# Result buffers, the order of additions and two small tables in a mixture-of-experts kernel

## The chip, the cores and the metric

One core of a Trainium2 chip runs the kernel. Its engines work side by side, each through its own instructions in order: TensorE (PE; the weight loads of its array are listed apart as PEld), VectorE (DVE), ScalarE (ACT), GpSimd (POOL) and SyncE (SP, which issues transfers). Sixteen DMA engines move data between the device memory and the on-chip memory. The metric is device time in microseconds (us), the median of several runs; less is better.

## The reference

A decoder layer over 1024 tokens of 1024 channels: a mixer (gated linear attention and a state-space layer side by side), then a mixture of experts in which each token goes to 4 of 32 experts. What the change touches is the second part:

```python
def moe_ffn(h, router_w, router_b, w_gu, b_gu, w_down, b_down):
    logits = (xt @ router_w + router_b)
    top_val, top_idx = lax.top_k(logits, TOP_K)            # 4 of 32
    gate = jax.nn.softmax(top_val, axis=-1)
    ...                                                    # tokens sorted by expert
    def expert_block(args):
        xblk, e = args
        gu = xblk @ w_gu[e] + b_gu[e]
        g, up = gu[:, :D_FF], gu[:, D_FF:]
        g = jnp.minimum(g, SWIGLU_LIMIT)
        up = jnp.clip(up, -SWIGLU_LIMIT, SWIGLU_LIMIT)
        act = (up + 1.0) * (g * jax.nn.sigmoid(SWIGLU_ALPHA * g))
        return act @ w_down[e] + b_down[e]
    yb = lax.map(expert_block, (xb, block_e)).reshape(cap, D_)
    out = jnp.zeros((N + 1, D_), f32).at[tok_buf].add(yb * w_buf[:, None])[:N]
```

The last line is the one to keep in mind: a token's result is the sum of four experts' results, each times its gate.

## The kernel before, in words

**Stages.** Up to about 600 us: mixer, router, and a list of tokens and gates for each expert in device memory. From 613 to 1957 us: the experts. After that the sums are read back, normalised and added to the input.

**Experts.** Each expert has a capacity that is fixed when the program is built, by the rank of its load (`CAPS`); blocks are of up to 128 of its tokens. The 32 experts are taken in eight groups of four. Of each group first the gate and up products run, 32 chunks of weights of 1 MB each, then the down products, 16 chunks. SP loads a chunk into one of six staging buffers; ScalarE makes its high f16 half (`split_hi`, L1585), VectorE its low half (`split_lo`, L1588), into one of seven slots. TensorE multiplies the high half by the high and the low half of the tokens (L1791, L1792) and the low half by the high one (L1800). Every VectorE split also writes one column of check values, `gacc`, and so do the splits of tokens (L148); L1894 adds the columns up at the end.

**Tokens.** POOL gathers a block's rows through its list (L1726, an indirect transfer from `hn_d`); TensorE transposes them (L1736), VectorE and ScalarE evict them as f16 halves. A group's tokens are fetched during the down products of the group before.

**Results.** The down products give results with channels on the partitions. `out_jobs` treats one block and one half of the channels (c = 0 or 1): TensorE transposes four tiles into one of two PSUM banks (L1759); ScalarE (L1602) or VectorE (L143) evicts the bank, times the gate, into one of the buffers `yt_r` (tile A7, so A in the rows); POOL issues an indirect transfer that adds the buffer's rows to the sums `ff_d[c]` in device memory (L1765). There are 102 such additions. A buffer is free when its addition has landed; an addition is ordered behind all earlier ones to the same `ff_d[c]`.

**The general path.** An expert with more tokens than its capacity is finished by a loop after the experts, which is not entered with this input. Two tables that say what that loop would have to do (`overflow_table`, L1478 to L1507) are made by some 17 small VectorE operations and three small products each, ahead of the first expert. At the very end of the expert stage `gacc` is reduced, the table entries are read by the engines and the loop's branch is not taken. Then the sums are loaded (L1980).

**What sets the order.** All the work of the expert stage is written as jobs. A `Job` has the engines that can do it with a cost each, a due number, the jobs that it must follow, and a lag (time between the end of its cost and its result). `run_jobs` is a greedy planner that runs when the program is built: it repeatedly takes the job that can start first, and among equals the one with the earliest due number, gives it to the engine that suits, and writes its instructions. So a change of costs, lags or of what a job follows changes the order of the instructions on all engines.

Of the kernel before, what the change touches and what calls it, by code (L numbers as in the profile page):

```python
# [17 lines left out]
OP = mybir.AluOpType  # L18
AX = mybir.AxisListType
# [29 lines left out]
def hybrid_layer_kernel(ctx: ExitStack, tc: tile.TileContext, I, out):  # L49
# [73 lines left out]
    def trb(*dims):  # L123
        return bank("tr", 2, *dims)
# [525 lines left out]
    def take(gen, n=1):  # L650
        for _ in range(n):
            try:
                next(gen)
            except StopIteration:
                return
# [680 lines left out]
    spacer = small(1)  # L1336
# [139 lines left out]
    ov, nb, starts, jf_, om, ent = small(32), small(32), small(32), small(1), small(32), small(2)  # L1476

    def overflow_table(i, cap):  # L1478
        nbt = view(63, 32, 8)
        if cap is None:  # L1480
            V.tensor_copy(ov, cr[:, 0:32])
        else:
            sub(ov, cr[:, 0:32], cap)
        tt(V, nbt, bc(ov, 2, 8), bc(k128, 1, 32), OP.is_gt)
        V.tensor_reduce(nb, nbt, axis=AX.X, op=OP.add)
        V.tensor_tensor_scan(ov, ones[:, 0:32], nb, 0.0, OP.mult, OP.add)
        sub(starts, ov, nb)
        tt(V, om, starts, ecol.to_broadcast([128, 32]), OP.is_le)
        tt(V, nb, ov, ecol.to_broadcast([128, 32]), OP.is_gt)
        mul(om, om, nb)  # L1490
        if cap is None:
            ts(starts, starts, -128.0, OP.mult)
        else:
            stt(starts, starts, -128.0, cap, OP.mult, OP.add)
        mul(nb, om, cr[:, 32:64])
        V.tensor_reduce(ent[:, 0:1], nb, axis=AX.X, op=OP.add)
        mul(nb, om, starts)
        V.tensor_reduce(ent[:, 1:2], nb, axis=AX.X, op=OP.add)
        stt(ent[:, 1:2], ecol, 128.0, ent[:, 1:2], OP.mult, OP.add)
        V.tensor_reduce(jf_, om, axis=AX.X, op=OP.add)  # L1500
        mul(ent[:, 1:2], ent[:, 1:2], jf_)
        yield
        pe3 = trb(130)
        for q in range(2):
            PE.matmul(pe3[0:1, 64 * q:64 * q + 64], ent[0:64, q:q + 1], ident[0:64, 0:64], start=True, stop=True)
        PE.matmul(pe3[0:1, 128:129], jf_, ones[:, 0:1], start=True, stop=True)
        V.tensor_copy(otf[0:1, i, 0:129], pe3[0:1, 0:129])  # L1507

    e2, e3 = slot("E2"), slot("E3")
# [9 lines left out]
        WL.append(carve(t_, 4, 4, 256).bitcast(F16))  # L1519
    NST, NWS = len(ST), len(WH)  # L1520
    a7 = slot("A7")
    yt_r = [carve(a7, 2 * i, 512) for i in range(3)]
    gacc = carve(a7, 6, 500)
    V.memset(gacc, 0.0)
    gs_r, u_t = [carve(e2, 0, 1024), carve(e2, 4, 1024)], carve(e3, 0, 1024)
    CG = max(sum(CAPS[r] for r in g) for g in GROUPS)
    XKB = CG * 32 / 1024
    X0, A0, Y0, XG0 = 0, XKB, 2 * XKB, 2 * XKB + 2 * CAPS[0] / 64
    assert XG0 + 12 <= 64, XG0
    xg_r = Ring([XG0, XG0 + 4, XG0 + 8], 1024)  # L1530
    n_acc = [0]
    NBS = [(c_ + 127) // 128 for c_ in CAPS]
# [1 line left out]
    RS = 1.0 / (WS * XS)  # L1534

    def acc_col():
        n_acc[0] += 1
        return gacc[:, n_acc[0] - 1:n_acc[0]]

    class Expert:  # L1540
        pass
# [206 lines left out]

    ot_free, yt_free, added, n_ot = [None] * 2, [None] * len(yt_r), [None] * 2, [0]

    def out_jobs(x, c, b, yT, due, after):
        cb = min(128, x.C - 128 * b)
        q, y = n_ot[0] % 2, n_ot[0] % len(yt_r)
        n_ot[0] += 1
        pt, yt = ot_[q], yt_r[y]

        def transpose(e):
            for k in range(4):
                PE.transpose(pt[0:cb, k], yT[:, k, 128 * b:128 * b + cb], ident)  # L1759
        t_ = Job({"PE": 0.46}, due, after + [ot_free[q]], transpose)  # L1760
        ot_free[q] = Job({"ACT": act_us(512, True), "DVE": dve_us(512)}, due + 2, [t_, yt_free[y]],
                         lambda e: scaled(e, yt[0:cb], pt[0:cb].rearrange("p a b -> p (a b)"),
                                          x.lt[0:cb, b, 1:2].bitcast(F32)))
        yt_free[y] = added[c] = Job({"POOL": 1.7}, due, [ot_free[q], added[c]],
                                    lambda e: P.indirect_dma_start(  # L1765
                                        out=ff_d[c], out_offset=bass.IndirectOffsetOnAxis(ap=x.lt[0:cb, b, 0:1], axis=0),
                                        in_=yt[0:cb], in_offset=None, compute_op=OP.add), lag=7.0)
        return t_


# [4 lines left out]
    def sub_jobs(i, kind, x, c, js, n):  # L1775
# [62 lines left out]
        else:  # L1838
# [13 lines left out]
            ev = Job({"ACT": act_us(nj * C, True, nj), "DVE": dve_us(nj * C, nj)}, due, [end] + wait, results)  # L1852
            evs.append(ev)
            if js[-1] == 3:
                place[2].extend(out_jobs(x, c, b, yT, due + 2, list(evs)) for b in range(x.NB))
                y_used.append(place)
        for q in bi:
            bank_free[q] = ev
# [3 lines left out]
    load_list(ex[GROUPS[0][0]])  # L1862
    biases()
    tables = [overflow_table(0, capr), overflow_table(1, None)]
    for t_ in tables:
        take(t_, 2)
    tr_ += [trb(4, 128) for _ in range(2)]
    flat = [(ex[r], b) for r in GROUPS[0] for b in range(NBS[r])]
    for n in range(2):
# [6 lines left out]
    for i, u in enumerate(subs):  # L1876
        while made < min(len(chunks) + 5, u[4] + 2):
            chunk_jobs(made)
            made += 1
        if i_ph % 2 and i_ph < len(phase) - 1 and phase[i_ph][1] == i:  # L1880
            todo = [(ex[r], b) for r in GROUPS[i_ph // 2 + 1] for b in range(NBS[r])]
            span_ = 2 * (phase[i_ph + 1][1] - i)
            for k, (x, b) in enumerate(todo):
                token_jobs(x, b, 2 * i + (span_ - 4) * k / len(todo), [ld[phase[i_ph - 1][0]], step[0]])
        if i_ph < len(phase) and phase[i_ph][1] <= i:
            i_ph += 1
        sub_jobs(i, *u)
    while made < len(chunks) + 5:
        chunk_jobs(made)
# [129 lines left out]
```

## Time and profile before

| | us |
|---|---|
| median of 3 runs (2018.4 to 2021.25) | 2021.15 |
| profiled execution | 2024.69 |
| its span, first to last instruction | 2022.9 |
| busy: PE, DVE, ACT, POOL | 1806.0, 1544.2, 1199.1, 526.5 |
| mean granted clock of TensorE, share of full speed | 0.948 |
| 102 additions, POOL's issue of them, in all | 260.7 |
| VectorE's low split of a chunk | 2.29 |
| ScalarE's high split of a chunk | 1.92 |

The profiled execution is one run, 0.2% above the median; what is read from its rows is set against its own time. Busy times of engines overlap, so they can't be added. What tells where an edit is felt is the idle time of an engine and what ended it, stage by stage.

### The profile page before, as it was taken

What the parts mean: (1) busy time and instruction counts of PE and PEld (TensorE: products, weight loads), DVE (VectorE), ACT (ScalarE), POOL (GpSimd) and SP (SyncE); (2) the same over time, 40 slices, a digit from 0 to 9 for tenths busy, and PEclk for the clock granted to TensorE, in tenths of its full rate; (3) what the DMA queues carried; (4) which work ended last, traced back from release to release, by engine and by line L of the source; (5) the groups of instructions that cost most, each with busy time, mean ns of one, the idle gap of its engine ahead of it and who ended that gap; (6) DMA issues with size and microseconds to landing.
All of it is one profiled execution on the core that took longest, in us unless ns stands there. A gap on an engine that the chain in (4) does not pass through costs nothing. (4 is left out here: it accounts for less than half of the span.)

```text
span 2022.9 us, 53263 instructions
## 1 busy us (share of the span) xinstructions
PE 1806.0 (89%) x22354; PEld 1614.5 (80%) x22354; DVE 1544.2 (76%) x2396; ACT 1199.1 (59%) x1682; POOL 526.5 (26%) x495
## 2 busy tenths in 40 slices
PE   8678699998968999998998899999899889999970
PEld 3566588787858999998998899767799789999870
DVE  5766537568767997995997799689799868869835
ACT  3524133544226876875776677577688667768641
POOL 4720012203543025015104402400330330160043
PEclk8889899999978999999999899999999989999985
DMA  9176465323359999999999899888999999999874
GB/s 310 39 193 132 137 196 161 126 70 131 115 172 326 363 322 353 379 351 307 323 329 358 278 351 341 279 323 301 299 367 365 301 296 330 327 318 350 306 192 175
DMA packets 296804, 540.82 MB, mean 267 GB/s; under 512 B 41234, under 2 KB 66032, under 8 KB 296528
## 3 DMA queue, kind: packets, MB, share of 16 engines
q1 hardware_dynamic: 259504, 469.51, 67.5%
q0 software_dynamic: 30384, 60.49, 11.8%
q10 hardware_dynamic: 6672, 7.38, 1.1%
q8 instruction: 177, 2.90, 0.6%
q14 instruction: 67, 0.55, 0.1%
HBM read 489.57 MB, written 45.61 MB: 265 GB/s over the span
## 5 line engine op out<-in xcount | busy, mean ns | idle before, releaser
L1765 POOL DMA_INDIRECT ff_d<-A,S x102 | 260.7, 2555 | 353.8 <-DVE A L143 141.2
L1588 DVE SCALAR_TENSOR_TENSOR B<-A,B 128x2048 f16<-128x2048 f32 x110 | 249.5, 2285 | 33.1 <-ACT B L1585 21.0
L1588 DVE SCALAR_TENSOR_TENSOR E<-A,E 128x2048 f16<-128x2048 f32 x110 | 249.7, 2285 | 16.0 <-ACT E L1585 15.8
L1726 POOL DMA_INDIRECT S<-hn_d,S x51 | 77.8, 1526 | 702.2 <-PE tr L1736 661.7
L1588 DVE SCALAR_TENSOR_TENSOR C<-A,C 128x2048 f16<-128x2048 f32 x110 | 249.7, 2284 | 8.3 <-ACT C L1585 8.2
L1585 ACT ACTIVATE B<-A 128x2048 f16<-128x2048 f32 x110 | 209.2, 1917 | 46.7 <-DMA A<-in_exp_w_gu_dram 36.7
L1585 ACT ACTIVATE E<-A 128x2048 f16<-128x2048 f32 x110 | 208.9, 1917 | 33.1 <-DMA A<-in_exp_w_gu_dram 18.4
L1585 ACT ACTIVATE C<-A 128x2048 f16<-128x2048 f32 x110 | 208.7, 1920 | 25.9 <-PE ax L1792 15.3
L1791 PE MATMUL mm<-S,E 128*128 128x92 f16 (+29 forms) x1336 | 187.8, 230 | 0.6 <-issue 0.5
L1791 PE MATMUL mm<-S,B 128*128 128x164 f16 (+28 forms) x1364 | 185.3, 227 | 3.3 <-issue 3.2
L1792 PE MATMUL mm<-S,B 128*128 128x164 f16 (+28 forms) x1364 | 184.9, 227 | 3.8 <-issue 3.8
L1792 PE MATMUL mm<-S,E 128*128 128x92 f16 (+29 forms) x1336 | 187.5, 229 | 0.0
L1792 PE MATMUL mm<-S,C 128*128 128x92 f16 (+28 forms) x1352 | 183.0, 226 | 3.2 <-issue 3.0
L1791 PE MATMUL mm<-S,C 128*128 128x92 f16 (+28 forms) x1352 | 183.2, 227 | 1.7 <-ACT S L1602 1.7
L1791 PEld LDWEIGHTS <-B 128*128 128x128 f16 x1760 | 154.3, 98 | 16.8 <-issue 9.4
L1791 PEld LDWEIGHTS <-C 128*128 128x128 f16 x1760 | 153.3, 98 | 13.0 <-issue 6.3
L1791 PEld LDWEIGHTS <-E 128*128 128x128 f16 x1760 | 155.0, 98 | 9.6 <-issue 2.0
L1792 PEld LDWEIGHTS <-B 128*128 128x128 f16 x1760 | 154.2, 98 | 9.4 <-issue 2.1
L1792 PEld LDWEIGHTS <-E 128*128 128x128 f16 x1760 | 154.9, 98 | 7.9 <-issue 0.4
L1792 PEld LDWEIGHTS <-C 128*128 128x128 f16 x1760 | 153.0, 98 | 8.3 <-issue 1.8
L148 DVE SCALAR_TENSOR_TENSOR S<-S 128x1 f32<-128x1 f32 (+7 forms) x249 | 106.0, 434 | 42.2 <-DMA S<-in_ada_w_dram 28.4
L1588 DVE SCALAR_TENSOR_TENSOR A<-A,A 128x2048 f16<-128x2048 f32 x54 | 123.5, 2286 | 3.1 <-ACT A L1585 2.9
(353 smaller groups left out, 4266.7 us busy)
## 6 DMA issues: line engine op xcount, KB each, us to landing
A<-in_exp_w_gu_dram SPq DMA_DIRECT2D x256, 1024.0 KB
A<-in_exp_w_down_dram SPq DMA_DIRECT2D x128, 1024.0 KB
S<-in_ada_w_dram POOLq DMA_DIRECT2D x64, 256.0 KB
S<-in_ada_w_dram SPq DMA_DIRECT2D x16, 512.0 KB
S<-in_w_in_dram SPq DMA_DIRECT2D x8, 1024.0 KB
S<-in_x_dram SPq DMA_DIRECT2D x12, 512.0 KB
ff_d<-S POOLq DMA_DIRECT2D x18, 256.0 KB
S<-in_w_out_dram SPq DMA_DIRECT2D x8, 512.0 KB
```

The source lines that it names most:

```text
L148: V.scalar_tensor_tensor(o, a, s, b, op0=op0, op1=op1, **kw)
L1585: A.activation(WH[n % NWS], ST[n % NST], AF.Copy, scale=WS)
L1588: V.scalar_tensor_tensor(WL[n % NWS], ST[n % NST], WS, WH[n % NWS], op0=OP.mult, op1=OP.subtract, accum_out=acc_col())
L1726: lambda e: P.indirect_dma_start(out=x_[0:cb], out_offset=None, in_=hn2_d, in_offset=bass.IndirectOffsetOnAxis(ap=x.lt[0:cb, b, 0:1], axis ...
L1765: lambda e: P.indirect_dma_start(out=ff_d[c], out_offset=bass.IndirectOffsetOnAxis(ap=x.lt[0:cb, b, 0:1], axis=0), in_=yt[0:cb], in_offset ...
L1791: PE.matmul(pp[q], w_, mh[:, f_], start=(f_ == 0 and q % per == 0), stop=False, skip_group_check=True)
L1792: PE.matmul(pp[q], w_, ml[:, f_], start=False, stop=False, skip_group_check=True)
```

## The change

Three things are changed. (1) There are seven result buffers instead of three: four in the tile A7, three behind the token buffers (tile S); the check values move out of A7 into a tile of their own with 256 columns, which are added into the first column when 255 are used. (2) Additions of the blocks of one expert to the same half are no longer ordered among themselves; a job follows the last addition before this expert (`was`) instead of the last addition (`added[c]`). A small memset on POOL stands ahead of every addition, and the planner's numbers for an addition go from 1.7 and a lag of 7 to 1.9 and 10. (3) The two tables of the general path are made by jobs at the start of the second group instead of ahead of the first expert. The diff, without the table's change of buffer, the check on sizes and where `put` is passed on:

```diff
-    yt_r = [carve(a7, 2 * i, 512) for i in range(3)]
-    gacc = carve(a7, 6, 500)
+    gacc = carve(e3, 7, 256)
...
+    yt_r = [carve(a7, 2 * i, 512) for i in range(4)] + [view(YT0 + 2 * i, 512) for i in range(3)]
...
     def acc_col():
+        if n_acc[0] == 255:
+            V.tensor_reduce(gacc[:, 0:1], gacc, axis=AX.X, op=OP.add)
+            n_acc[0] = 0
         n_acc[0] += 1
-        return gacc[:, n_acc[0] - 1:n_acc[0]]
+        return gacc[:, n_acc[0]:n_acc[0] + 1]
...
-    def out_jobs(x, c, b, yT, due, after):
+    def out_jobs(x, c, b, yT, due, after, was, prev):
...
-        yt_free[y] = added[c] = Job({"POOL": 1.7}, due, [ot_free[q], added[c]],
-                                    lambda e: P.indirect_dma_start(
-                                        out=ff_d[c], out_offset=bass.IndirectOffsetOnAxis(ap=x.lt[0:cb, b, 0:1], axis=0),
-                                        in_=yt[0:cb], in_offset=None, compute_op=OP.add), lag=7.0)
+        def put(e):
+            P.memset(spacer, 0.0)
+            a_ = P.indirect_dma_start(out=ff_d[c], out_offset=bass.IndirectOffsetOnAxis(ap=x.lt[0:cb, b, 0:1], axis=0),
+                                      in_=yt[0:cb], in_offset=None, compute_op=OP.add)
+            for o_ in prev:
+                tc.declare_no_dep(a_.ins, o_.ins, reason="each token is in an expert's list once")
+            prev.append(a_)
+        yt_free[y] = added[c] = Job({"POOL": 1.9}, due, [ot_free[q], was], put, lag=10.0)
...
-                place[2].extend(out_jobs(x, c, b, yT, due + 2, list(evs)) for b in range(x.NB))
+                was, prev = added[c], []
+                place[2].extend(out_jobs(x, c, b, yT, due + 2, list(evs), was, prev) for b in range(x.NB))
...
     tables = [overflow_table(0, capr), overflow_table(1, None)]
-    for t_ in tables:
-        take(t_, 2)
...
+        if i == phase[2][1]:
+            for q, t_ in enumerate(tables):
+                u_free[0] = Job({"DVE": 4.0}, 2 * i, [u_free[0]], lambda e, t_=t_: take(t_))
+                p_ = Job({"PE": 1.0}, 2 * i, [u_free[0], tr_free[q]], lambda e, t_=t_: take(t_))
+                tr_free[q] = Job({"DVE": 0.3}, 2 * i, [p_], lambda e, t_=t_: take(t_))
```

The order of instructions at three places follows; L1765 of before is L1771 now, L1726 is L1731, L1588 is L1593. First POOL at the end of the expert stage, before: the last six additions and the first row behind them. `ff_d_748` and `ff_d_749` are the two halves of the sums, A_4732 the tile with the buffers; the names behind "waits" are the semaphores that a row waits for, those with DMASW of transfers that POOL issued.

```order
L1765 DMA ff_d_748<-A_4732,S 1152x512 [waits DMASW1_49,DVE_49]
L1765 DMA ff_d_749<-A_4732,S 1152x512 [waits DMASW2_49,Activation_49]
L1765 DMA ff_d_748<-A_4732,S 1152x512 [waits DMASW3_49]
L1765 DMA ff_d_749<-A_4732,S 1152x512 [waits DMASW4_49,Activation_49]
L1765 DMA ff_d_748<-A_4732,S 1152x512 [waits DMASW5_49,Activation_49]
L1765 DMA ff_d_749<-A_4732,S 1152x512 [waits DMASW6_49]
L1906 TENSOR_LOAD S [waits DVE_49]
```

And now, the last six additions with the memsets between them:

```order
L1771 DMA ff_d_748<-S 1152x512 [waits DMASW1_49,DVE_49]
L1770 MEMSET S 128x1 [waits Pool_49]
L1771 DMA ff_d_748<-S 1152x512 [waits DVE_49]
L1770 MEMSET S 128x1 [waits Pool_49]
L1771 DMA ff_d_749<-A_4732,S 1152x512 [waits DMASW5_49,DMASW2_49,DVE_49]
L1770 MEMSET S 128x1 [waits Pool_49]
L1771 DMA ff_d_749<-A_4732,S 1152x512 [waits DVE_49]
L1770 MEMSET S 128x1 [waits Pool_49]
L1771 DMA ff_d_748<-A_4732,S 1152x512 [waits DMASW7_49,DMASW4_49,Activation_49]
L1770 MEMSET S 128x1 [waits Pool_49]
L1771 DMA ff_d_749<-A_4732,S 1152x512 [waits DMASW6_49,DVE_49]
```

Before, the two halves alternate and each row waits for an earlier transfer; now the two blocks of an expert's half stand one behind the other, and the second does not wait for a transfer. Of all 102 additions 101 waited for a transfer of POOL's before, and 79 do now.

VectorE where the expert stage begins, before: the copies of the experts' biases (L1614, L143), then the first rows of the first table, of which 34 stand ahead of the first low split.

```order
L1614 COPY E_4724<-tr 128x256 [waits PE_49]
L143 TENSOR_SCALAR E_4724<-tr 128x256
L1614 COPY E_4724<-tr 128x256 [waits PE_49]
L139 TENSOR_TENSOR S<-S 128x32 [waits DVE_49]
L130 TENSOR_TENSOR S<-S 128x256 [waits DVE_49]
L1485 TENSOR_REDUCE S<-S 128x32 [waits DVE_49]
L1486 SCALAR_TENSOR_TENSOR S<-S 128x32 [waits DVE_49]
```

And now:

```order
L1524 MEMSET E_4724 128x256
L1619 COPY E_4724<-tr 128x256 [waits PE_49]
L143 TENSOR_SCALAR E_4724<-tr 128x256
L1619 COPY E_4724<-tr 128x256 [waits PE_49]
L1593 SCALAR_TENSOR_TENSOR B_4573,E_4724<-A_4725,B_4573 128x2048 [waits DMAHW7_49,DVE_49,Activation_49]
L1593 SCALAR_TENSOR_TENSOR B_4574,E_4724<-A_4726,B_4574 128x2048 [waits DMAHW4_49,Activation_49]
```

The splits of the first two chunks now follow the bias copies directly. The tables' rows stand on VectorE between the last chunks of the first group and the first ones of the second: one table ahead of the split of that group's first chunk (into A_4731), one behind it.

POOL at the change from the fifth group to the sixth, before: additions 51 to 53 of the 102, and between them the last three gathers of the sixth group's tokens.

```order
L1765 DMA ff_d_748<-A_4732,S 1152x512 [waits DMASW3_49,DVE_49]
L1765 DMA ff_d_748<-A_4732,S 1152x512 [waits DMASW1_49,DVE_49]
L1726 DMA S<-hn_d,S 128x1024 [waits DMAHW7_49,DMASW6_49,PE_49]
L1726 DMA S<-hn_d,S 120x1024 [waits DMASW7_49,DMASW4_49,PE_49]
L1726 DMA S<-hn_d,S 48x1024 [waits DMAHW0_49,DMASW0_49,PE_49]
L1765 DMA ff_d_748<-A_4732,S 1152x512 [waits DMASW2_49,Activation_49]
```

And now the same three gathers, from addition 57 on:

```order
L1771 DMA ff_d_749<-A_4732,S 1152x512 [waits DMASW7_49,Activation_49]
L1770 MEMSET S 128x1 [waits Pool_49]
L1771 DMA ff_d_749<-A_4732,S 1152x512 [waits DMASW0_49,Activation_49]
L1731 DMA S<-hn_d,S 128x1024 [waits DMAHW7_49,DMASW1_49,PE_49]
L1770 MEMSET S 128x1 [waits Pool_49]
L1771 DMA ff_d_748<-A_4732,S 1152x512 [waits DMASW4_49,DMASW2_49,DVE_49]
L1731 DMA S<-hn_d,S 120x1024 [waits DMASW3_49,PE_49]
L1731 DMA S<-hn_d,S 48x1024 [waits DMAHW0_49,PE_49]
```

They stood behind 52 additions and now stand behind 58 and 59.

## Rows read from the trace of the kernel before

**Rows 1.** Windows: stretch, its length, busy (count) of PE, PEld, DVE, ACT, POOL; clock, DMA share, GB/s.

```profile
613.00:1957.00 1344.00, 1282.37 (x19165) 1195.28 (x19165) 1123.68 (x1412) 952.41 (x1164) 314.42 (x142) 0.98 0.97 326
780.00:943.00 163.00, 157.22 (x2409) 156.09 (x2407) 141.56 (x176) 125.69 (x158) 40.36 (x20) 1.00 1.03 352
```

**Rows 2.** Waits of PE, 613 to 1957 us: who, for what: us in total, times, longest.

```profile
PE ax L1759 <- DVE A L143: 18.5, 7, 6.1
PE ax L1759 <- ACT A L1602: 15.7, 3, 12.4
...
PE mm L1800 <- DVE E L1588: 2.0, 2, 1.2
```

**Rows 3.** Waits over the whole span, those for additions to land.

```profile
ACT A L1602 <- DMA ff_d<-A,S: 103.9, 24, 13.0
...
POOL ff_d L1765 <- DMA ff_d<-A,S: 86.0, 23, 8.5
...
DVE A L143 <- DMA ff_d<-A,S: 31.0, 10, 8.1
```

**Rows 4.** Timeline, 1606 to 1624 us: start, length, engine, line, operation, [idle before <- releaser].

```profile
1606.32 2.02 POOL L1765 DMA_INDIRECT ff_d<-A,S  x1 [0.30 <-issue]
...
1622.15 0.68 ACT L1602 ACTIVATE A<-ax,S 4x512 f32<-4x512 f32 x1 [8.16 <-DMA ff_d<-A,S]
...
1622.88 1.06 PE L1759 MATMUL ax<-S 128*60 128x128 f32 x4 [12.40 <-ACT A L1602]
```

**Rows 5.** Windows, five stretches at half clock: the last of them, and the sum.

```profile
1622.90:1625.60 2.70, 2.70 (x24) 2.51 (x25) 0.00 (x0) 2.27 (x6) 2.11 (x2) 0.50 1.05 269
sum 17.10, PE 17.09 PEld 15.65 DVE 13.16 ACT 7.04 POOL 12.81; mean PE 3.42 PEld 3.13 DVE 2.63 ACT 1.41 POOL 2.56
```

**Rows 6.** Timeline, 1928 to 1986 us, the end of the expert stage.

```profile
1928.79 3.36 POOL L1765 DMA_INDIRECT ff_d<-A,S  x1 [103.57 <-DVE A L143]
...
1958.06 0.67 DVE L1894 TENSOR_REDUCE S<-A 128x1 f32<-128x500 f32 x1
...
1958.43 0.55 PE L1800 MATMUL mm<-S,E 128*128 128x36 f16 x16
...
1977.43 1.40 POOL L1765 DMA_INDIRECT ff_d<-A,S  x1 [1.29 <-DMA ff_d<-A,S]
...
1983.66 2.14 SPq L1980 DMA_DIRECT2D S<-ff_d  x4
```

**Rows 7.** Timeline, around 1124 us: one issue of an addition on POOL.

```profile
1123.95 8.82 POOL L1765 DMA_INDIRECT ff_d<-A,S  x1 [0.30 <-issue]
```

**Rows 8.** Timeline, 593 to 605 us: the tables and the first splits.

```profile
593.86 0.18 DVE L139 TENSOR_TENSOR S<-S 128x32 f32<-128x32 f32 x1
...
600.38 1.91 ACT L1585 ACTIVATE B<-A 128x2048 f16<-128x2048 f32 x1 [6.92 <-DMA A<-in_exp_w_gu_dram]
...
600.87 0.37 PE L1505 MATMUL tr<-S 64*1 64x64 f32 x2 [2.95 <-DVE S L1496]
...
602.45 2.27 DVE L1588 SCALAR_TENSOR_TENSOR B<-A,B 128x2048 f16<-128x2048 f32 x1
```

**Rows 9.** Timeline, 763 to 780 us: the second group's first splits and first product.

```profile
763.00 2.29 DVE L1588 SCALAR_TENSOR_TENSOR A<-A,A 128x2048 f16<-128x2048 f32 x1
...
770.28 2.29 DVE L1588 SCALAR_TENSOR_TENSOR B<-A,B 128x2048 f16<-128x2048 f32 x1 [4.98 <-ACT B L1585]
...
779.98 0.24 PE L1791 MATMUL mm<-S,A 128*128 128x184 f16 x1
```

**Rows 10.** Groups by line, POOL: operation, count | busy us, mean ns | idle before, releaser.

```profile
L1765 POOL DMA_INDIRECT ff_d<-A,S x102 | 260.7, 2555 | 353.8 <-DVE A L143 141.2
...
L1408 POOL MEMSET S<- 128x1 f32 x32 | 3.6, 112 | 0.1
```

**Rows 11.** Timeline: a gather at 1438.91 us, and PE's first product of that expert.

```profile
1438.91 1.01 POOL L1726 DMA_INDIRECT S<-hn_d,S  x1 [6.69 <-PE tr L1736]
...
1483.98 0.23 PE L1791 MATMUL mm<-S,C 128*128 128x148 f16 x1
```

More of the change, by code (lines that the diff above doesn't have):

```diff
@@ L1478, in overflow_table @@
     def overflow_table(i, cap):
-        nbt = view(63, 32, 8)
+        nbt = u_t[:, 0:256].rearrange("p (r b) -> p r b", b=8)
         if cap is None:
@@ L1502, in overflow_table @@
         yield
-        pe3 = trb(130)
+        pe3 = tr_[i].rearrange("p a b -> p (a b)")[:, 0:130]
         for q in range(2):
@@ L1506, in overflow_table @@
         PE.matmul(pe3[0:1, 128:129], jf_, ones[:, 0:1], start=True, stop=True)
+        yield
         V.tensor_copy(otf[0:1, i, 0:129], pe3[0:1, 0:129])
@@ L1528, in hybrid_layer_kernel @@
     X0, A0, Y0, XG0 = 0, XKB, 2 * XKB, 2 * XKB + 2 * CAPS[0] / 64
-    assert XG0 + 12 <= 64, XG0
+    YT0 = XG0 + 12
+    yt_r = [carve(a7, 2 * i, 512) for i in range(4)] + [view(YT0 + 2 * i, 512) for i in range(3)]
+    assert YT0 + 6 <= 68.5, YT0
     xg_r = Ring([XG0, XG0 + 4, XG0 + 8], 1024)
```

## The prediction

> **What bounds the kernel now.** I read the busy shares by stretch first, because the page's shares are averages over several stages. The expert stage runs from 613 to 1957 us, two thirds of the span. There TensorE is busy in 1282.4 of 1344 us, VectorE in 1123.7, ScalarE in 952.4, POOL in 314.4 [rows 1]. Next I read what ends TensorE's idle time in that stage. Weights are hardly ever late: the longest such item, the wait of the low products for the VectorE split, is 2.0 us in all. The two large items are at L1759, the transposes of results: 18.5 us behind VectorE's eviction and 15.7 us behind ScalarE's [rows 2], together 34.2 of 61.6 us idle. The third view asks why the evictions are late: ScalarE waits 103.9 us for additions into ff_d to land and VectorE 31.0, while POOL itself waits 86.0 us between additions [rows 3]. So the chain is: addition lands, its buffer comes free, the eviction that stood first on its engine runs, a PSUM bank comes free, TensorE goes on. One instance in full: an addition issued at 1606.32, the eviction that wants its buffer only at 1622.15, and TensorE, stopped for 12.4 us, at 1622.88 [rows 4]. From issue to buffer free that is 15.8 us.
>
> A stall costs more than itself. In the five stretches that follow the longest stalls the granted clock is 0.50 to 0.51, the lower of the two levels (1.2 instead of 2.4 GHz), and 17.1 us of products run there [rows 5]. At full clock they would take half, so 8.5 us more hang on the stalls: 34.2 + 8.5 = 42.7 us.
>
> The last twelve additions are a second place. They run one by one from 1928.79 to 1977.43, 48.6 / 11 = 4.4 us apart, the loads of ff_d start at 1983.66, 6.2 us after the last, and the last products of the experts are at 1958.43 [rows 6]. So some 20 us of the end are additions alone.
>
> **Seven buffers, and additions that don't wait for each other (stage).** An eviction waits for the addition seven before it, not three. At the tail's 4.4 us each, seven take 31 us, more than the longest landing of [rows 4], so a single late landing no longer reaches TensorE. The second part shortens the line itself, but not by much: in the new order 79 of the 102 additions still wait for an earlier transfer (101 before), since additions of different experts stay ordered. And the issue is not always short: one took 8.82 us while VectorE was splitting [rows 7], against 1.4 in the tail. So I keep three quarters of 42.7, 32 us. The upper end is all of it, 42.7. The lower end is 22: if bursts of slow issues fill seven buffers as three are filled now, only the two longest of the ten waits go, 12.4 and 6.1 us [rows 2], with two of the five stretches at half clock: 18.5 + 2/5 x 8.5. Is there something next in line? The DMA engines are at 0.97 over the stage, and at 1.03 in a stretch where TensorE is busy for 157.2 of 163 us [rows 1]; 1344 x (1 - 0.97 / 1.03) = 78 us are free before they bind, so weights still arrive in time.
>
> **The tail.** Additions of one expert's half go out together, so a half's chain has one link for an expert instead of one for a block. After the last products (1958.43 and some 3 us for evicting, transposing and evicting again, about 1961.6) I count two links of at most 6.2 us [rows 6]: loads at about 1974 instead of 1983.66, 10 us. Bounds: 14 (one link and a half), 4 (three and a half). What comes after those loads does not change.
>
> **Tables moved (start).** They hold VectorE from 593.86 to 602.45, 8.6 us, ahead of the first low split. But the second chunk's high split ends at 600.38 + 1.91 = 602.3 and had waited for its transfer [rows 8], which no part of the change moves, and its low split follows the first at 604.7. In the new order the first split is done by then, and the second begins 2.4 us earlier. I take 2.4; the bounds are 0 (if the tokens' transfers end last) and 8.6.
>
> **Tables in their new place.** Two batches of 17 small VectorE operations, 8.6 us, stand around the split at 763.00. The next low split is at 770.28 and TensorE begins on the new group's weights at 779.98, 14.7 us after the first split ends at 765.3 [rows 9]. So 8.6 us fit below that lead; if the cover were gone they would cost 8.6. TensorE's own part is two times 0.37 us and a shorter product [rows 8], 0.9 in all, and that is on the path. The check values' extra reduction is half the width of the final one, whose 0.67 us [rows 6] is its upper bound on VectorE. Together -1.5.
>
> **Memsets.** 102 at 0.11 us are 11 us of POOL [rows 10]. In the stage POOL is idle for three quarters of the time, so they are hidden; in the tail four of them lie on the chain, 0.4 us, inside the tail's bounds. The higher cost and lag given to the planner (1.9 and 10 us) move rows but add no work.
>
> **Sum.** 32 + 10 + 2.4 - 1.5 = 43 us. The profiled execution took 2024.7 us, span 2022.9; that gives 1981.7. The median of the runs shown is 2021.15, 3.5 lower, so the time forecast is 2021.15 - 43 = **1978 us**.
>
> **The rivals.**
>
> *POOL becomes the bound of the line.* 102 additions take 260.7 us of POOL, 2.56 us each [rows 10], and with 11 us of memsets and the gathers the issue itself can't be spread. For it: the 8.82 us issue [rows 7], and that additions now come in bursts of up to six. Against it: POOL is busy for only 314 of 1344 us [rows 1]. Then half of the stalls stay: 21 + 5 + 2.4 - 1.5 = 27 us, 1994.
>
> On how such an issue gets slow, the Trainium skill ("SBUF — State Buffer", section "SBUF: two separate sides") says that transfers started from GpSimd have their descriptors written by its own cores, and that VectorE, when it holds the port pair that both share, keeps GpSimd from writing them. The trace agrees so far as one issue beside splits took 8.82 us and those in the tail 1.4. By that rule more buffers would not shorten an issue, and the time would be this rival's.
>
> *The order frees nearly nothing.* 79 of 102 additions still wait, and a chain that is slower than its producers fills any ring. Then the tail and little else remain: 10 + 2.4 - 1.5 = 11 us, 2010. Against it: between additions POOL has long idle time (353.8 us ahead of them in all [rows 10]), so on average the line drains.
>
> *Slower: gathers behind additions.* At the change from the fifth group to the sixth, the gathers for one expert of the next group stood behind 52 additions and now stand behind 58 and 59. Before, they were issued at 1438.91 and later, and TensorE came to that expert's first product at 1483.98 [rows 11], some 40 us after; about 10 of these go to landing, transposes and splits. With X us for an addition on the queue, TensorE would wait 7X - 30. At 4.4 that is 1 us. It decides against the change above (30 + 43) / 7 = 10.4 us each. At 15.8 each, as in [rows 4], it is 80 us, net 37 slower: 2058.
>
> **How the numbers follow.** Forecast as worked out: 0.68, with a range from 1961 (42.7 + 14 + 4 - 0.9 = 60 us gained) to 1997 (22 + 4 + 0 - 2 = 24). POOL the bound: 0.17, 1986 to 2003. Little freed: 0.08, 2003 to 2021, of which 0.03 within 0.2%, which is 4 us and about what a measurement of this kernel can tell from no change. Gathers late: 0.07, above 2025. The range 1961 to 2003 leaves out the last two cases and a little below, 0.15 to 0.2. Faster 0.90, same 0.03, slower 0.07.
>
> **What would show it.** In the changed kernel's profile: waits of TensorE at the result transposes under 10 us in the stage; waits of ScalarE and VectorE for ff_d under 40 us together; no long stretch at half clock after 700 us but at stalls of another kind; ff_d's loads at most 17 us after the last products; the first low product 2 us earlier than now; the tables' rows near 765 us with no wait of TensorE beside them. It would be wrong if waits of the token transposes for gathers appear at the later group changes, if additions cluster at 5 to 15 us of issue and the result transposes still wait, or if weights become late and the low products wait for their splits by more than 20 us.

## The result and the profile after

| | us | ratio to before, 95% interval |
|---|---|---|
| before, median of 4 runs | 2021.2 | |
| changed, median of 4 runs (5297.41 to 5316.23) | 5303.88 | 2.6235 (2.615 to 2.632) |
| profiled execution of the changed kernel, its span | 5297.9 | |

The forecast was 1978. The time is 2.6 times that of before, so something runs that did not run then. The page shows where. Its first part (busy time of each engine, share of the span, instructions) and the rows by 40 slices:

```profile
span 5297.9 us, 102101 instructions
...
PE 4175.5 (79%) x42003; PEld 3926.2 (74%) x42003; DVE 1974.0 (37%) x3776; ACT 1551.5 (29%) x2557; POOL 723.9 (14%) x744
...
PE   7899899999999976777777777777777777777774
...
PEclk8999899999999988888888888888888888888887
```

TensorE has 42003 products in place of 22354. The first 14 of 40 slices look like the kernel before; from then on the slices are all alike. Two stretches by windows (columns as in [rows 1]): the expert stage from its first to its last product, and what follows it; behind them the same stage of the kernel before.

```profile
615.18:1914.14 1298.96, 1268.84 (x19228) 1186.98 (x19225) 1134.82 (x1450) 953.64 (x1162) 312.80 (x237) 0.99 1.00 338
1933.00:5256.00 3323.00, 2377.43 (x19649) 2314.22 (x19649) 426.36 (x1372) 355.44 (x882) 202.44 (x147) 0.85 0.66 201
...
613.73:1958.98 1345.25, 1283.11 (x19216) 1196.04 (x19213) 1124.43 (x1413) 952.41 (x1164) 314.90 (x142) 0.98 0.97 326
```

The stage is 1299 us long; before, it was 1345.3. It has become shorter by 46 us. Behind it stand 3323 us of other work. The groups by line name that work (columns as in [rows 10]): L1932 is the gather and L1948 the gate and up product of the general path's loop.

```profile
L1948 PE MATMUL mm<-S,B 128*128 128x128 f32 x4704 | 639.8, 299 | 0.0
L1932 POOL DMA_INDIRECT S<-hn_d,S x49 | 48.7, 994 | 420.3 <-DMA S<-L_d 413.3 <-DMA S<-in_exp_b_gu_dram 7.0
```

The loop that is not entered before runs 49 times here. The timeline of its two ends (the last addition of the expert stage, the loop's first load, the loads of the sums):

```profile
1927.19 1.42 POOL L1771 DMA_INDIRECT ff_d<-A,S  x1 [2.67 <-DMA ff_d<-A,S]
...
1933.59 0.37 SPq L1976 DMA_DIRECT2D S<-L_d  x1
...
5256.05 2.27 SPq L1993 DMA_DIRECT2D S<-ff_d  x4
```

The account closes: from 1933.59 to 5256.05 are 3322.5 us, 67.8 for a turn. The sums were loaded at 1983.66 before [rows 6], so up to the loop the kernel is 50.1 us earlier, and 3322.5 - 50.1 = 3272.4 is what the loads came later. In the stage, the waits of TensorE at the result transposes [rows 2] are nearly gone; this is the row that answers to them, and the one for additions that POOL itself waits for [rows 3], over the time up to the loop:

```profile
PE ax L1764 <- DVE A L143: 0.5, 1, 0.5
...
POOL ff_d L1771 <- DMA ff_d<-A,S: 36.5, 10, 9.0
```

**Why the loop runs.** Its count is the last entry of the first table. The two tables share two small tiles: `ent` (the entries) and `jf_` (the count), allocated once outside `overflow_table`. VectorE fills them, TensorE copies them into the table's row. Before, each table was made whole: fill, copy, fill, copy. Now there are jobs, and the second fill follows the first fill but not the first copy. The timeline of the changed kernel between 771 and 784 us (L1500 and L133 end a table's fill, L1481 begins the second one, L1505 and L1506 are the copies):

```profile
771.76 0.18 DVE L1500 TENSOR_REDUCE S<-S 128x1 f32<-128x32 f32 x1
771.98 0.16 DVE L133 TENSOR_TENSOR S<-S 128x1 f32<-128x1 f32 x1
...
774.28 0.18 DVE L1481 COPY S<-S 128x32 f32<-128x32 f32 x1
...
777.41 0.18 DVE L1500 TENSOR_REDUCE S<-S 128x1 f32<-128x32 f32 x1
777.62 0.16 DVE L133 TENSOR_TENSOR S<-S 128x1 f32<-128x1 f32 x1
...
780.44 0.38 PE L1505 MATMUL tr<-S 64*1 64x64 f32 x4
...
780.87 0.38 PE L1505 MATMUL tr<-S 64*1 64x64 f32 x4
```

Both copies come after the second fill, so both rows of the table hold the second one, the list of all blocks, made for the case in which the fast path's results can't be used. The first, what goes over the capacities, is empty here. 49 turns fit that: the capacities make 51 blocks (102 additions, two for each), the actual loads a little fewer. Every token's result is so added a second time in f32. By the code, the RMS norm behind the sums divides by their own size, so twice the sums give nearly the same layer, and the time is what shows it.

### The profile page after: what moved, and what is told of

Same layout as the page of the kernel before. It is cut to its first block, busy times and chain, and to the rows that moved or that the text cites. A ratio compares the mean times of both kernels' runs of the same rounds, so it can differ in the third digit from the quotient of the medians.

```text
span 5297.9 us, 102101 instructions
## 1 busy us (share of the span) xinstructions
PE 4175.5 (79%) x42003; PEld 3926.2 (74%) x42003; DVE 1974.0 (37%) x3776; ACT 1551.5 (29%) x2557; POOL 723.9 (14%) x744
## 5 line engine op out<-in xcount | busy, mean ns | idle before, releaser
L1948 PE MATMUL mm<-S,B 128*128 128x128 f32 x4704 | 639.8, 299 | 0.0
L1948 PEld LDWEIGHTS mm<-S,B 128*128 128x128 f32 x4704 | 618.3, 215 | 16.2 <-DVE S L1938 16.2
L1963 PE MATMUL mm<-S,E 128*128 128x128 f32 x4704 | 562.3, 276 | 31.8 <-DMA E<-in_exp_w_down_dram 31.8
L1963 PEld LDWEIGHTS mm<-S,E 128*128 128x128 f32 x4704 | 540.7, 192 | 41.1 <-DMA E<-in_exp_w_down_dram 41.1
L1948 PE MATMUL mm<-S,C 128*128 128x128 f32 x4704 | 557.3, 275 | 0.0
L145 DVE TENSOR_SCALAR E<-mm,S 128x128 f32<-128x128 f32 x392 | 137.5, 351 | 1107.8 <-PE mm L1948 1107.8
L1948 PEld LDWEIGHTS mm<-S,C 128*128 128x128 f32 x4704 | 541.0, 192 | 0.0
L1969 POOL DMA_INDIRECT ff_d<-A,S x98 | 153.7, 1569 | 2700.7 <-ACT A L1607 2700.7
L1982 PE MATMUL tr<-S 24*128 24x24 f32 x49 | 13.1, 268 | 584.4 <-DMA S<-in_exp_b_down_dram 584.4
L1937 PE MATMUL tr<-S 128*128 128x128 f32 x392 | 96.5, 427 | 324.4 <-DMA S<-hn_d,S 324.4
L1964 ACT ACTIVATE S<-mm,S 128x128 f32<-128x128 f32 x294 | 108.1, 368 | 533.9 <-PE mm L1963 533.9
L1593 DVE SCALAR_TENSOR_TENSOR B<-A,B 128x2048 f16<-128x2048 f32 x110 | 249.8, 2285 | 21.6 <-ACT B L1590 21.4
L1593 DVE SCALAR_TENSOR_TENSOR E<-A,E 128x2048 f16<-128x2048 f32 x110 | 249.8, 2286 | 19.8 <-ACT E L1590 19.6
L1593 DVE SCALAR_TENSOR_TENSOR C<-A,C 128x2048 f16<-128x2048 f32 x110 | 249.8, 2286 | 15.1 <-ACT C L1590 14.9
```

The lines of the kernel that those rows point to most:

```text
L145: (e or V).tensor_scalar(o, a, s1, s2, op0=op0, op1=op1)
L1593: V.scalar_tensor_tensor(WL[n % NWS], ST[n % NST], WS, WH[n % NWS], op0=OP.mult, op1=OP.subtract, accum_out=acc_col())
L1937: PE.transpose(pt[:, k], x_[:, 128 * (4 * hf + k):128 * (4 * hf + k) + 128], ident)
L1948: PE.matmul(pp_[q], SF[q + 2 * (c % 2)][:, k, 128 * j:128 * j + 128], xT[:, k], start=(k == 0), stop=(k == 7))
L1963: PE.matmul(pd, st[:, k, 128 * j:128 * j + 128], aT[:, k], start=(k == 0), stop=(k == 7))
L1964: A.activation(yT[:, 2 * (c % 2) + j], pd, AF.Identity, bias=bias[16 + 2 * c + j])
```

## The experiments

Theory: the shared tiles. Rival A: the check values, which moved and are now folded at 255 columns, are no longer finite, so the whole general path is asked for. Rival B: an input of the tables is overwritten by one of the new result buffers before they are made, since they are made later. The trace speaks against A already: with check values that are not finite the code would first write zeros over the sums (the memset of L1923, then eight turns of stores), and no such row stands between the last addition at 1927.19 and the loop's first load at 1933.59.

### The second fill behind the first copy

```diff
+            p_ = None
             for q, t_ in enumerate(tables):
-                u_free[0] = Job({"DVE": 4.0}, 2 * i, [u_free[0]], lambda e, t_=t_: take(t_))
+                u_free[0] = Job({"DVE": 4.0}, 2 * i, [u_free[0], p_], lambda e, t_=t_: take(t_))
```

> The changed kernel, but VectorE's part of the second table waits for TensorE's part of the first. Theory (shared entries): both tables are written into the same two small tiles; in the changed order TensorE copies the first table only after VectorE has put the second there, so the loop is given the table of all 49 blocks, runs 49 times and adds everything once more. With this wait the loop is not entered. Its time then follows from the changed kernel's trace up to there: last addition issued at 1927.2 us instead of 1977.4, 50 us less, so 2021 - 50 = 1971 us, between 1963 and 1980. Rival A (check values): the columns of check values, moved and folded, give something that is not finite, so the whole general path is taken: this edit leaves them as they are, and the time stays near 5300. Rival B (a small input of the tables is overwritten by the new result buffers before they are made): also near 5300.

Measured: 1975.97 us median, ratio 0.9757 (0.9726 to 0.9787). The loop is gone. Its timeline has the order that the theory asks for: the first copy at 776.29, the second fill from 777.16 on, the second copy at 785.14.

```profile
776.29 0.38 PE L1505 MATMUL tr<-S 64*1 64x64 f32 x4
...
777.16 0.16 DVE L1481 COPY S<-S 128x32 f32<-128x32 f32 x1
...
780.34 0.18 DVE L1500 TENSOR_REDUCE S<-S 128x1 f32<-128x32 f32 x1
...
785.14 0.38 PE L1505 MATMUL tr<-S 64*1 64x64 f32 x4
```

### The kernel before, with only the copies moved behind both fills

```diff
     for t_ in tables:
-        take(t_, 2)
+        take(t_)
+    for t_ in tables:
+        take(t_)
```

> The kernel before, with nothing changed but the order of four steps at the start: VectorE's part of both tables, then TensorE's part of both. Theory (shared entries): the first table is again given the second one's entries, the loop runs 49 times at (5304 - 1971) / 49 = 68 us: 2021 + 49 x 68 = 5350 us, between 5300 and 5400. Rivals A and B: neither the check values nor the result buffers are touched, so 2021.

Measured: 5346.95 us in one execution. Four steps in another order, with three buffers, the old check values and ordered additions, give the whole loss. The gathers of the loop, in the groups by line:

```profile
L1921 POOL DMA_INDIRECT S<-hn_d,S x49 | 48.7, 994 | 414.0 <-DMA S<-L_d 407.0 <-DMA S<-in_exp_b_gu_dram 7.0
```

This alone rules out both rivals as needed causes; the first run, which leaves check values and buffers as the change has them, rules them out as causes of their own.

### The tables ahead of the first expert

```diff
+    for t_ in tables:
+        take(t_, 3)
...
-        if i == phase[2][1]:
-            for q, t_ in enumerate(tables):
...
```

> The changed kernel with both tables made ahead of the first expert, each whole, as before; seven buffers, unordered additions and the moved check values stay. Theory (shared entries): no loop; against the mended kernel 2.4 us more at the start (0 to 8.6) and about 1 less at the second group, so 1973 us, between 1963 and 1982. Rival A (check values): near 5300. Rival B (inputs overwritten): 1973 too.

Measured: 1974.17 us, ratio 0.9751 (0.972 to 0.9783). No loop, so the check values and the additions are innocent. The place of the tables makes no difference that shows beside the mended kernel.

### Two tiles for each table

```diff
-    ov, nb, starts, jf_, om, ent = small(32), small(32), small(32), small(1), small(32), small(2)
+    ov, nb, starts, om = small(32), small(32), small(32), small(32)
+    own_ = [(small(1), small(2)) for _ in range(2)]
...
     def overflow_table(i, cap):
+        jf_, ent = own_[i]
```

> The changed kernel, its order of jobs as it is, but each table has its own two small tiles for entries and count. Theory (shared entries): the order does no harm any more, no loop, as the mended kernel: 1971 us, between 1963 and 1980, and within 4 us of it. Rival A (check values) and rival B (inputs overwritten): near 5300.

Measured: 1975.45 us, ratio 0.9763 (0.9733 to 0.9794). The order of jobs is not changed at all here. So it is the sharing of the two tiles in this order that does the harm, not the place or the order as such. The tables' new scratch buffer (`u_t`) is kept by all of these kernels but the second and does no harm either.

The cause of the 5304 us is settled by these four. The other eight ask where the 46 us come from that the mended kernel gains, against the terms of the prediction.

### Three buffers, or ordered additions, in the mended kernel

```diff
+    del yt_r[3:]
     ot_free, yt_free, added, n_ot = [None] * 2, [None] * len(yt_r), [None] * 2, [0]
```

> The mended kernel with three result buffers again; everything else of the change stays. Theory (the ring of buffers takes the stalls away): an eviction again waits for the addition three before it, and TensorE again stops at the result transposes; unordered additions and the longer lag in the plan help a little, so 20 to 40 us of the mended kernel's 46 are lost: 2005 us, between 1994 and 2018, with 15 to 35 us of waits at L1764. Rival (the order of the additions does it): within 5 us of the mended kernel, 1971 to 1981.

Measured: 1995.73 us, ratio 0.9867 (0.9843 to 0.989); 17.0 us of waits at the transposes for ScalarE, up to the stage's last products. The theory's direction, the near end of its size: some 20 of the 46 us are lost.

```diff
-            for o_ in prev:
-                tc.declare_no_dep(a_.ins, o_.ins, reason="each token is in an expert's list once")
-            prev.append(a_)
-        yt_free[y] = added[c] = Job({"POOL": 1.9}, due, [ot_free[q], was], put, lag=10.0)
+        yt_free[y] = added[c] = Job({"POOL": 1.9}, due, [ot_free[q], added[c]], put, lag=10.0)
```

> The mended kernel with seven buffers, but every addition again ordered behind all earlier ones to the same half. Theory (buffers for the stage, order for the end): the stage keeps its gain, under 5 us of waits at L1764, and the end loses what it won, 5.3 us by the profiles (25.2 us from the last products to the loads of ff_d before, 19.9 mended), so 1981 us, between 1976 and 1988. Rival (the order does it): 2005 to 2020, with the waits at L1764 back.

Measured: 1999.55 us, ratio 0.9859 (0.9833 to 0.9886). Both expectations missed: more is lost than the theory had (1976 to 1988) and less than the rival (2005 to 2020), and one wait of 11.2 us at the transposes is back. These two runs undo one part each in a kernel with the other edits, so both parts were also tried alone.

### Each part alone

Seven buffers alone: the kernel with the tables first, additions ordered, without memsets, the planner's old numbers.

```diff
-            P.memset(spacer, 0.0)
...
-            for o_ in prev:
-                tc.declare_no_dep(a_.ins, o_.ins, reason="each token is in an expert's list once")
-            prev.append(a_)
-        yt_free[y] = added[c] = Job({"POOL": 1.9}, due, [ot_free[q], was], put, lag=10.0)
+        yt_free[y] = added[c] = Job({"POOL": 1.7}, due, [ot_free[q], added[c]], put, lag=7.0)
```

> The kernel before with seven result buffers (and the check values moved and folded for that); tables first, additions ordered, no memsets, the planner's old numbers. Theory (buffers and order share the same stalls; from the run with seven buffers and ordered additions, 24 us below before): 1998 us, between 1990 and 2005, one or two waits of TensorE for a late landing left. Rival (buffers do all of the stage, and the rest there came from the moved tables): 1980 to 1986.

Measured: 1987.96 us, ratio 0.9826 (0.9804 to 0.9848), between the two. 34 us of the gain are the buffers' alone. The run before it has seven buffers and ordered additions too, but the tables moved, the memsets and the planner's new numbers, and was only 24 us below its own baseline; where the 10 us between the two go was not followed.

Unordered additions alone: the kernel with the tables first, and three buffers, by the same line as above (`del yt_r[3:]`).

> The changed kernel with the tables ahead of the first expert and three result buffers: additions of one expert's half unordered, memsets, the planner's new numbers. Theory (as the mended kernel with three buffers, 28 us below before, and the tables' place costs nothing): 1995 us, between 1988 and 2002, with 10 to 20 us of waits at the result transposes. Rival (with three buffers the place of the tables matters, as in the run that moved them alone, 12.6 us slower): 1978 to 1986.

Measured: 2003.88 us, ratio 0.9901 (0.9884 to 0.9918): 18 us, less than either expectation. Windows from the first to the start of the last product, and, over the whole span, the waits of TensorE at the result transposes and of POOL for landings; first seven buffers alone:

```profile
618.24:1924.85 1306.61, 1271.18 (x19214) 1186.96 (x19212) 1130.67 (x1418) 950.47 (x1159) 313.26 (x141) 0.99 0.99 335
...
PE ax L1764 <- DVE A L143: 7.9, 2, 7.4
...
POOL ff_d L1770 <- DMA ff_d<-A,S: 81.0, 21, 8.9
```

and unordered additions alone:

```profile
619.64:1952.20 1332.56, 1281.76 (x19198) 1194.24 (x19196) 1122.38 (x1414) 955.84 (x1164) 302.34 (x238) 0.98 0.97 329
...
PE ax L1765 <- ACT A L1607: 19.6, 8, 4.6
...
PE ax L1765 <- DVE A L143: 7.9, 3, 3.6
...
POOL ff_d L1772 <- DMA ff_d<-A,S: 19.5, 8, 7.7
```

The two parts work on different waits. With buffers alone POOL still waits for landings as before (81.0 us against 86.0 [rows 3], and 48.6 more for additions from the new buffers), but TensorE hardly feels it: one wait of 7.4 us and a short one. With the order alone POOL's waits fall to 19.5 us and TensorE's longest from 12.4 to 4.6 us, but eleven waits of up to that length stay. The two gains, 34 and 18, add up to a little more than the 45 to 49 us of both together, so the parts overlap by a few us at most.

### The tables alone, in the kernel before

The mended jobs for the tables, with three buffers, ordered additions and the old check values.

> The kernel before, with only the two tables moved to the second group and the second one's VectorE part behind the first one's TensorE part. Theory by the prediction's terms: 2.2 us earlier at the first product, about 1 us of TensorE later, and 4.3 us of new waits right behind the first products as the mended kernel's profile has them: within 6 us of before, 2017 to 2028. Rival (the new place costs more, since VectorE is then busy with splits and evictions): 2030 or more.

Measured: 2035.87 us, ratio 1.0062 (1.0038 to 1.0086), so slower by 12.6 us; the rival. Its timeline shows one place, on POOL, ScalarE and TensorE:

```profile
793.23 12.56 POOL L1766 DMA_INDIRECT ff_d<-A,S  x1 [2.84 <-DVE A L143]
...
811.47 0.69 ACT L1603 ACTIVATE A<-ax,S 108x512 f32<-108x512 f32 x1 [14.46 <-DMA ff_d<-A,S]
...
814.62 0.31 PE L1792 MATMUL mm<-S,B 128*128 128x180 f16 x1 [6.40 <-ACT E L1603]
```

An addition took 12.56 us to issue; ScalarE, which in this order has the eviction, stood 14.46 us for its landing, with the next split and the evictions of finished products queued behind it, and TensorE waited 6.4 us. In the stage TensorE's idle time is 75.0 us here and 62.1 before; this place is 6.4 of the 12.9, the waits at the result transposes are 3.4 more. The rest was not followed, and that the move made this issue long is not shown: the kernel before has one of 15.05 us.

### The memset, and the planner's numbers

The kernel before with a memset ahead of each addition:

```diff
+        def put(e):
+            P.memset(spacer, 0.0)
+            P.indirect_dma_start(out=ff_d[c], out_offset=bass.IndirectOffsetOnAxis(ap=x.lt[0:cb, b, 0:1], axis=0),
+                                 in_=yt[0:cb], in_offset=None, compute_op=OP.add)
```

> The kernel before with only a memset on POOL ahead of each addition. In the profiles with the memsets they take 0.58 us each and the longest issue of an addition is 7 to 9 us, while without them it is 12 to 15 us. Theory (the memset only adds its time on an engine with room): 2021 to 2027, with some issues of 12 us or more still there. Rival (the memset takes a wait off the issue and so shortens the longest ones): 2005 to 2018, longest issue under 10 us, fewer waits at L1759.

Measured: 2025.71 us, ratio 1.0011 (0.9989 to 1.0034): no effect, and the waits at the transposes are 34.3 us (20.0 and 14.3) against 34.2. The longest issue is 11.0 us, between the two expectations; it does not move the time.

The old numbers (1.7, lag 7) for an addition, first in the mended kernel, then with the tables first:

```diff
-        yt_free[y] = added[c] = Job({"POOL": 1.9}, due, [ot_free[q], was], put, lag=10.0)
+        yt_free[y] = added[c] = Job({"POOL": 1.7}, due, [ot_free[q], was], put, lag=7.0)
```

> The mended kernel with the planner's numbers for an addition as before (1.7 and a lag of 7 instead of 1.9 and 10). Theory (the numbers only shift rows; seven buffers cover landings of either length): within 4 us of the mended kernel, 1971 to 1980. Rival (the longer lag is what keeps evictions from being planned too early): waits at L1764 of 10 us or more and 1985 or more.

> The changed kernel with the tables ahead of the first expert and the planner's old numbers for an addition (1.7, lag 7): the two edits that each gave about 2 us below the mended kernel, together. Theory (both differences are noise): 1974 us, between 1969 and 1980. Rival (they are real and add up): 1968 to 1972.

Measured: 1974.01 us, ratio 0.9767 (0.9743 to 0.979), and 1976.86 us, ratio 0.9781 (0.9763 to 0.9799). The numbers make no difference, and the small differences between the mended kernels don't add up. Five versions stand between 1974 and 1977 us; all beat both kernels of the comparison by 2.2 to 2.5% and 63%, and which of them is best can't be told.

## Why the prediction was wrong, step by step

The forecast gain was 43 us and the mended kernel gains 46, which is in part luck, as the terms below show: the stage's was too small, the tail's and the start's too large. But the changed kernel as it is runs 3283 us longer. One step of the prediction carries that.

**The tables' new place: the step that failed.** It priced two batches of VectorE operations, set them against the lead of the splits, and added two copies on TensorE. All of that is about when, nothing about what is in the tile when it is read. Yet the diff, which the prediction had at hand, holds the fault: the second fill's list of predecessors has the first fill and not the first copy, so both fills may stand ahead of both copies, as they do from 771.76 to 780.87. The question that was not asked is which tile the second fill writes and who still has to read it. Before, program order answered it; in jobs only the listed predecessors do, and the first copy is not among them. The transfers' and engines' waits are then built for the order that the planner wrote, so nothing stops and nothing is late. What the runs showed in place of the term of -1.5 us: a first table with the second one's entries and 49 turns of the loop at 67.8 us each; with one more predecessor, or two tiles for each table, no turn at all.

**A rival that was missing.** "The change doesn't do what it says" was worked out as stalls that stay. It should have had its second reading: a moved step that computes something else, on which a branch hangs. The price could have been bounded from the code: up to 51 blocks, each with an expert's twelve chunks of weights (1024 KB each) loaded again, which at the stage's 326 GB/s [rows 1] is an estimate of 39 us for each, some 2000 us in all.

**What bounds the kernel.** Right: 34.2 us of waits at the result transposes became 0.5, and the clock in the stage rose from 0.98 to 0.99. The stage's length by profile, from the first product to the start of the last row of them:

| kernel | stage | last product to loads of the sums | ratio of medians |
|---|---|---|---|
| before | 1344.7 | 25.2 | 1 |
| unordered alone | 1332.6 | 19.5 | 0.9901 |
| buffers alone | 1306.6 | 23.3 | 0.9826 |
| both, tables first | 1297.3 | 20.1 | 0.9751 |
| both, mended | 1305.3 | 19.9 | 0.9757 |

**The stage's term, 32 us.** Too small: 47 with the tables first, 39 mended, and 46 in the changed kernel itself, up to its loop. The discount of a quarter rested on 79 of 102 additions that still wait for an earlier transfer. That number told nothing: POOL's waits for landings fell from 86.0 to 31.6 us in the mended kernel. It is the order that shortens them, for with buffers alone they are 81.0 and 48.6. A likely reason, not tested by itself, is that what a row waits for lies further back and has mostly landed. How long a wait is can't be read from how many rows have one. The full 42.7 would have been the better value. The other part that was off is the clock's. The prediction took five stretches at half clock, 17.1 us of products, and so 8.5 us. The stage has ten, with 40.7 us, and the changed kernel four, with 14.5; half of the difference is 13.1 us. The sums over all stretches of the stage with a granted clock of 0.50: before, buffers alone, unordered alone, changed.

```profile
sum 52.87, PE 40.71 PEld 35.23 DVE 32.76 ACT 23.75 POOL 21.41; mean PE 4.07 PEld 3.52 DVE 3.28 ACT 2.38 POOL 2.14
sum 26.88, PE 20.55 PEld 15.76 DVE 17.22 ACT 13.22 POOL 6.79; mean PE 4.11 PEld 3.15 DVE 3.44 ACT 2.64 POOL 1.36
sum 51.47, PE 42.66 PEld 35.01 DVE 31.33 ACT 29.92 POOL 27.89; mean PE 4.74 PEld 3.89 DVE 3.48 ACT 3.32 POOL 3.10
sum 16.96, PE 14.50 PEld 12.96 DVE 12.15 ACT 10.57 POOL 3.52; mean PE 3.62 PEld 3.24 DVE 3.04 ACT 2.64 POOL 0.88
```

The stage's windows agree: of the 46 us that it became shorter, TensorE's idle time gave 32.0 (62.1 to 30.1) and its busy time, for as many products, 14.3 (1283.1 to 1268.8). Unordered additions alone bring the idle time to 50.8 us but leave as much work at the lower clock as before; the buffers take half of it away. In single profiles this part varies: it is 25.4 us of products in the mended kernel and 14.1 with the tables first, and half of that difference is 5.7 of the 8 us between their stages. The weights did arrive in time, as the step on the DMA engines said: their share is 1.00 in the changed stage.

**The tail, 10 us.** Measured 5.3. Two links were counted after the last product; in the mended kernel six additions still come behind it, 1.9 us apart by POOL alone as long as they don't wait. The rows, from the last product on:

```profile
1916.17 0.55 PE L1809 MATMUL mm<-S,E 128*128 128x36 f16 x16
...
1917.28 1.58 POOL L1771 DMA_INDIRECT ff_d<-S  x1 [1.71 <-DMA ff_d<-A,S]
1919.17 1.62 POOL L1771 DMA_INDIRECT ff_d<-S  x1 [0.19 <-issue]
...
1921.13 1.58 POOL L1771 DMA_INDIRECT ff_d<-A,S  x1 [0.23 <-issue]
1923.02 1.60 POOL L1771 DMA_INDIRECT ff_d<-A,S  x1 [0.19 <-DMA ff_d<-S]
1925.71 1.40 POOL L1771 DMA_INDIRECT ff_d<-A,S  x1 [0.98 <-issue]
1929.81 1.42 POOL L1771 DMA_INDIRECT ff_d<-A,S  x1 [2.58 <-DMA ff_d<-A,S]
```

Once the links between transfers are short, POOL's own issue is the next in line, and the sum had no term for it; one landing, of 2.58 us, still adds to it.

**The start, 2.4 us, and the -1.5.** The first product came at 610.86 in the mended kernel, but the biases' transposes ahead of it also began earlier; from them to the first product it is 27.9 us against 29.9, so 2.0. Right behind stand two waits, 1.67 and 2.65 us, that the kernel with the tables first does not have; the kernel before has one such, of 1.71 us, at 650.66:

```profile
634.09 0.20 PE L1800 MATMUL mm<-S,E 128*128 128x96 f16 x1 [1.67 <-ACT S L1607]
...
636.94 0.24 PE L1801 MATMUL mm<-S,E 128*128 128x96 f16 x1 [2.65 <-DVE S L148]
```

They take back what the start won: TensorE comes sooner to tokens that are not split yet. From 634.88 to 641.71, between and behind them, the granted clock is 0.50. The term was right in size and was no gain: even without its fault, moving the tables brought nothing that the times show.

**Rivals.** POOL as the bound: no. The longest issues are still 5 to 8 us in the mended kernel, but seven buffers cover them. So the rule of the Trainium skill that was weighed there ("SBUF — State Buffer", section "SBUF: two separate sides") decides nothing about the time here. In the trace of the kernel before, slow issues and low splits do coincide: splits ran on VectorE during 0.81 of the time of the eight additions that took 4 us or more to issue (up to 15.05 us, so the prediction's 8.82 was not the longest), and during 0.30 of the time of the 43 under 2 us that were issued before 1900 us; they fill 0.65 of the stage. But nothing was changed to test this, whether these splits hold that port pair no run here shows, and the cause of the slow issues stays open. Gathers late: no, from the first product on TensorE waits 1.2 us in all at the token transposes of the changed kernel. A shift of rows that makes things slower did show in the run that moved the tables alone, with three buffers: 12.6 us, but not by this rival's way, for TensorE waits 0.9 us at the token transposes in that stage.

## What to carry to other kernels

When steps that stood in program order are turned into jobs, write down for each moved step what it writes, who still has to read that, and whether the planner knows; two uses of one small tile are two jobs with an edge between them, or two tiles. A branch that a profile shows as not taken has a price all the same: work out what it would cost and what decides it before calling an edit to its inputs free. And for a ring of buffers, set the longest time from issue to landing against the ring's length; a count of rows that still wait says little.

## What was not expected of the hardware

The memset ahead of an addition takes 0.58 us in the trace (102 in 59.1 us on POOL) against 0.11 for the same shape elsewhere [rows 10], and yet costs no time; its rows overlap with those of the issue ahead of it. The groups by line of the changed kernel:

```profile
L1770 POOL MEMSET S<- 128x1 f32 x102 | 59.1, 579 | 0.0
```

The first product of the experts came between 605 and 620 us in the profiles of kernels whose work ahead of it is nearly the same. A difference of a few us between the times of one event in two single profiles is therefore no evidence; the time from one event to another in the same profile can be.
